# A batched A·Bᵀ kernel: the stores wait for one load more, and the last two batches are stored from the SP queue

## The chip, the cores and the metric

One core of a Trainium2 chip runs the program. The metric is the time of one execution in device microseconds (us); a median of several runs is given.

## The reference

```python
batch, m, k, n = 16, 512, 512, 512          # float32 inputs a, b from randn
def reference(a, b):
    return np.matmul(a, b.transpose(0, 2, 1)).astype(np.float32)
```

33.55 MB are read and 16.78 MB written. The work inside is done in bf16.

## The kernel before

The kernel works on pairs of batches. A load brings `a` or `b` of one pair (2 MB), so there are 16 loads, 0 to 15; a store takes the product of one batch (1 MB), so there are 16 stores, 0 to 15. There are seven slots for loads and seven for outputs (`ob`). VectorE casts to bf16, TensorE transposes and multiplies, ScalarE copies the transposed `a` and the products. SP issues all loads; GpSimd (POOL in the profile) issues all stores, after a first wait for a load.

```python
    STORES = "SSSSOSOSOSSOSOSOSOSOSOSSS"      # S: issue a store; O: wait for one, tell ScalarE
    ...
        for n in range(NL):
            load(n)
        for n in range(2 * pairs):            # SP: relay each landing, issue a later load
            got = nc.sync.wait_ge(s_ld[n % NL], 16 * (n // NL + 1))
            ...
            if n > 0 and n + NL - 1 < 2 * pairs:
                load(n + NL - 1)
        for n in range(batch - NO, batch - 1):
            nc.sync.wait_ge(s_st[n % NO], 16 * (n // NO + 1))

        n_st = n_of = 0
        nc.gpsimd.wait_ge(s_ld[6], 16)        # load 6 has landed: stores may start
        for what in STORES:
            if what == "S":
                slot = n_st % NO
                nc.gpsimd.wait_ge(s_out, n_st + 1)        # ScalarE has copied batch n_st
                nc.gpsimd.dma_start(
                    out[n_st].rearrange("(p j) n -> p j n", j=J), ob[:, slot]
                ).then_inc(s_st[slot], 16)
                n_st += 1
            else:
                nc.gpsimd.wait_ge(s_st[n_of % NO], 16 * (n_of // NO + 1)).then_inc(s_of, 1)
                n_of += 1
    ...
        # ScalarE, per pair: copies of the transposed a, then for each batch e of the pair
                take(s_of, 1)                             # a free slot of ob
                ...                                       # four copies ob <- ps
    ...
    with tc.tile_critical(no_gpsimd_drain=True):
        nc.sync.wait_ge(s_st[(batch - 1) % NO], 16 * ((batch - 1) // NO + 1))
```

Of the kernel before, what the change touches and what calls it, by code (L numbers as in the profile page):

```python
# [10 lines left out]
def kernel(  # L11
# [6 lines left out]
    nc = tc.nc  # L18
    P = 128
    batch, M, K = a.shape  # L20
    _, N, _ = b.shape
    J = M // P
# [7 lines left out]
    NO = 7  # L30


    STORES = "SSSSOSOSOSSOSOSOSOSOSOSSS"

    def sbuf(name, shape, dtype):
        return ctx.enter_context(nc.sbuf_tensor(name, shape, dtype))

    def sem(name):
        return tc.alloc_semaphore(name)

    with tc.tile_critical(no_gpsimd_drain=True):  # L41
# [8 lines left out]
        ob = sbuf("ob", [P, NO, J, N], f32)  # L50
# [3 lines left out]
        s_set = sem("s_set")  # L54
        s_ld = [sem(f"s_ld{i}") for i in range(NL)]
        s_second = [sem(f"s_second{i}") for i in range(2)]
        s_st = [sem(f"s_st{i}") for i in range(NO)]

        s_go = sem("s_go")
# [13 lines left out]
        s_out = sem("s_out")  # L73
# [5 lines left out]
            out=ident[:], in_=ident[:], compare_op=mybir.AluOpType.not_equal, fill=1.0,  # L79
# [7 lines left out]
        def load(n):  # L87
            u, slot = n // 2, n % NL
            src = (a if n % 2 == 0 else b)[2 * u:2 * u + 2].rearrange(
                "e (p j) k -> (e p) j k", j=2 * J  # L90
            )
            if n >= NL:

                nc.sync.wait_ge(s_cd, n - NL + 2)
            if n < 2:
                nc.sync.dma_start(
                    ld[:, slot, :J, :], src[:, :J, :]
                ).then_inc(s_ld[slot], 16)
                nc.sync.dma_start(
                    ld[:, slot, J:, :], src[:, J:, :]  # L100
                ).then_inc(s_second[slot], 16)
            else:
                nc.sync.dma_start(ld[:, slot], src).then_inc(s_ld[slot], 16)
# [3 lines left out]
        for n in range(2 * pairs):  # L107
# [6 lines left out]

            if n > 0 and n + NL - 1 < 2 * pairs:
                load(n + NL - 1)
        for n in range(batch - NO, batch - 1):
            nc.sync.wait_ge(s_st[n % NO], 16 * (n // NO + 1))


        n_st = n_of = 0
        nc.gpsimd.wait_ge(s_ld[6], 16)
        for what in STORES:
            if what == "S":
                slot = n_st % NO
# [20 lines left out]
        with nc.Fori(0, pairs, engines=[dve]) as u:  # L146
            for x, (h, w, s_c, s_w) in enumerate(
# [4 lines left out]
                if x == 0:  # L152
# [3 lines left out]
                    out=h[:, :J, :], in_=src[:, :J, :HK]  # L156
# [4 lines left out]
                    out=h[:, J:, :], in_=src[:, J:, :HK]  # L161
                ).then_inc(s_c, 1)
                nc.vector.tensor_copy(  # L163
                    out=w[:, J:, :], in_=src[:, J:, HK:]
                ).then_inc(s_w, 1)
            for ko in range(KO):
# [5 lines left out]
                if ko == 1:  # L172
# [3 lines left out]
                    out=tb[:, ko, :],  # L176
# [9 lines left out]
        with nc.Fori(0, pairs, engines=[act]) as u:  # L186
            for ko in range(KO):
# [5 lines left out]
                for e in range(2):  # L193
                    c = nc.scalar.copy(  # L194
                        out=ta[:, ko, e * J * P:(e + 1) * J * P].rearrange(
                            "k (j p h) -> k j p h", j=J, h=2
                        ),
# [5 lines left out]
            for e in range(2):  # L203
                take(s_of, 1)
                dst = ob[:, bass.ds((u * 2 + e) % NO, 1)].rearrange("m o j n -> m (o j) n")
                for j in range(J):
                    if j < J - 1:
                        nc.scalar.wait_ge(s_mm, j + 1)
                    else:
# [3 lines left out]
                        out=dst[:, j, :].rearrange("m (p j) -> m p j", j=2 * J),  # L213
# [51 lines left out]


    with tc.tile_critical(no_gpsimd_drain=True):
        nc.sync.wait_ge(s_st[(batch - 1) % NO], 16 * ((batch - 1) // NO + 1))


# [28 lines left out]
```

## Time and profile before

| | before |
|---|---|
| time, median (range) | 126.12 us (125.92 to 126.35) |
| span of the profile | 124.6 us |
| TensorE, VectorE, ScalarE busy | 75%, 56%, 55% |
| transfer rate, mean of the span | 404 GB/s |
| last landing of a store | 123.02 us |

The prediction below shows the rows of the page that carry the argument. The list of waits gives the rest of GpSimd's story; its columns are the total in us, how often, and the longest.

```profile
POOL out_dram L127 <- DMA out_dram<-ob: 59.3, 9, 10.2
POOL out_dram L127 <- DMA ld<-in_a_dram: 36.8, 1, 36.8
POOL out_dram L127 <- ACT ob L212: 10.1, 2, 8.5
```

GpSimd waits once for a load (the hold), then for its own stores, because only four or five may be under way, and at the end twice for ScalarE. That last row is the only place where a store waits for compute.

### The profile page before, as it was taken

The numbers are of one execution on the slowest core, as the hardware profiler recorded it, in microseconds if no ns is written. First come the engines' busy times: TensorE is split into PE (matmuls) and PEld (weight loads), VectorE is DVE, ScalarE is ACT, GpSimd is POOL, SyncE is SP. The second block draws the span as 40 slices with busy tenths as digits, with TensorE's granted clock in tenths as the row PEclk, the third lists the DMA queues.
The fourth block names the chain that finished last, engine by engine and source line by source line (L and its number), as shares of the span: only waits on it lengthen the run. The fifth ranks groups of instructions, "written<-read, shape, count | busy, mean of one in ns | idle before, by whom it ended". The sixth has DMA issues, their size and how long they took to land. (4 is left out here: it accounts for less than half of the span.)

```text
span 124.6 us, 2416 instructions
## 1 busy us (share of the span) xinstructions
PE 93.2 (75%) x768; PEld 58.8 (47%) x768; DVE 70.4 (56%) x112; ACT 68.3 (55%) x130; POOL 10.7 (9%) x22
## 2 busy tenths in 40 slices
PE   0005199998999999899989965999389992899300
PEld 0005295467447644754674445844286451734000
DVE  0055677758983895686689139590687608830000
ACT  4004234589468855956795682645906666456300
POOL 2000000000006200100003020010101001200300
PEclk9999999999999999999999998699959999999995
DMA  3999999999999999999999999999999999999790
GB/s 79 397 437 429 447 426 437 442 421 431 421 426 421 400 442 413 418 447 410 455 410 423 450 402 460 408 426 447 418 437 421 434 413 434 421 423 429 316 381 8
DMA packets 4896, 50.33 MB, mean 404 GB/s; under 512 B 544, under 2 KB 544, under 8 KB 544
## 3 DMA queue, kind: packets, MB, share of 16 engines
q1 hardware_dynamic: 2592, 33.56, 63.9%
q0 software_dynamic: 2304, 16.78, 32.0%
HBM read 33.55 MB, written 16.78 MB: 404 GB/s over the span
## 5 line engine op out<-in xcount | busy, mean ns | idle before, releaser
L254 PE MATMUL ps<-tb,ta 128*128 128x512 bf16 x256 | 57.7, 379 | 0.4
L212 ACT COPY ob<-ps 128x512 f32 x64 | 34.7, 587 | 26.1 <-PE ps L254 26.1
L194 ACT COPY ta<-tp 128x512 bf16<-128x512 bf16 x64 | 32.9, 604 | 21.5 <-PE tp L235 21.5
L254 PEld LDWEIGHTS ps<-tb,ta 128*128 128x128 bf16 x256 | 24.1, 98 | 30.5 <-issue 3.9
L235 PE MATMUL tp<-ident,ha 128*128 128x128 bf16 x256 | 20.8, 241 | 12.6 <-PEq L136 12.6
L235 PE MATMUL tp<-ident,hb 128*128 128x128 bf16 x256 | 19.5, 237 | 10.0 <-PEq L136 9.9
L235 PEld LDWEIGHTS tp<-ident,ha 128*128 128x128 bf16 x256 | 18.2, 109 | 15.6 <-issue 14.0
L175 DVE COPY tb<-tp 128x1024 bf16<-128x1024 bf16 x32 | 21.4, 686 | 5.5 <-DVEq L136 5.4
L235 PEld LDWEIGHTS tp<-ident,hb 128*128 128x128 bf16 x256 | 17.3, 108 | 10.9 <-issue 10.9
L127 POOL DMA_DIRECT2D out_dram<-ob x16 | 10.0, 628 | 106.2 <-DMA out_dram<-ob 59.3
L155 DVE CAST hb<-ld 128x1024 bf16 x8 | 5.6, 699 | 16.8 <-DVEq L136 16.8
L170 DVE COPY ha<-wa 128x2048 bf16<-128x2048 bf16 x8 | 5.5, 694 | 8.0 <-DVEq L136 7.6
L155 DVE CAST ha<-ld 128x1024 bf16 x8 | 5.5, 690 | 6.8 <-DVEq L136 6.7
L160 DVE CAST hb<-ld 128x1024 bf16 x8 | 5.5, 684 | 1.1 <-DVEq L136 1.1
L160 DVE CAST ha<-ld 128x1024 bf16 x8 | 5.5, 686 | 1.0 <-DVEq L136 1.0
L174 DVE COPY hb<-wb 128x2048 bf16<-128x2048 bf16 x8 | 5.5, 686 | 0.5 <-DVEq L136 0.5
L158 DVE CAST wb<-ld 128x1024 bf16 x8 | 5.6, 694 | 0.0
L158 DVE CAST wa<-ld 128x1024 bf16 x8 | 5.5, 688 | 0.0
L163 DVE CAST wa<-ld 128x1024 bf16 x8 | 5.5, 687 | 0.0
L163 DVE CAST wb<-ld 128x1024 bf16 x8 | 5.5, 684 | 0.0
L185 ACT ACT_TABLE_LOAD x1 | 1.3, 1283 | 1.1 <-SPq L41 1.1
L78 POOL TENSOR_SCALAR_AFFINE_SELECT ident<-ident 128x128 bf16<-128x128 bf16 x1 | 0.3, 284 | 0.2 <-POOL ident L76 0.2
(6 smaller groups left out, 0.8 us busy)
## 6 DMA issues: line engine op xcount, KB each, us to landing
out_dram<-ob POOLq DMA_DIRECT2D x16, 1024.0 KB, 23.9
ld<-in_a_dram SPq DMA_DIRECT2D x7, 2048.0 KB, 33.0
ld<-in_b_dram SPq DMA_DIRECT2D x7, 2048.0 KB, 33.7
ld<-in_a_dram SPq DMA_DIRECT2D x2, 1024.0 KB, 6.3
ld<-in_b_dram SPq DMA_DIRECT2D x2, 1024.0 KB, 10.4
```

What stands on the lines that cost most here:

```text
L127: nc.gpsimd.dma_start(out[n_st].rearrange("(p j) n -> p j n", j=J), ob[:, slot]).then_inc(s_st[slot], 16)
L155: nc.vector.tensor_copy(out=h[:, :J, :], in_=src[:, :J, :HK]).then_inc(s_cd, 1)
L158: nc.vector.tensor_copy(out=w[:, :J, :], in_=src[:, :J, HK:])
L160: nc.vector.tensor_copy(out=h[:, J:, :], in_=src[:, J:, :HK]).then_inc(s_c, 1)
L163: nc.vector.tensor_copy(out=w[:, J:, :], in_=src[:, J:, HK:]).then_inc(s_w, 1)
L170: nc.vector.tensor_copy(out=ha[:], in_=wa[:]).then_inc(s_ca, 1)
L174: nc.vector.tensor_copy(out=hb[:], in_=wb[:]).then_inc(s_cb, 1)
L175: nc.vector.tensor_copy(out=tb[:, ko, :], in_=tp[:, 2 + ko % 2].rearrange("k j p -> k (j p)"),).then_inc(s_eb, 1)
L194: c = nc.scalar.copy(out=ta[:, ko, e * J * P:(e + 1) * J * P].rearrange("k (j p h) -> k j p h", j=J, h=2), in_=tp[:, ko % 2, :, e * HP:(e ...
L212: c = nc.scalar.copy(out=dst[:, j, :].rearrange("m (p j) -> m p j", j=2 * J), in_=ps[:, j, :].rearrange("m (j p) -> m p j", j=2 * J),)
L235: t = nc.tensor.transpose(tp[:, 2 * x + g, j, :], h[:, j, g * P:(g + 1) * P], ident[:])
L254: t = nc.tensor.matmul(ps[:, j, :], ta[:, ko, (e * J + j) * P:(e * J + j + 1) * P], tb[:, ko, :].rearrange("k (j p) -> k j p", j=2 * J)[:, ...
```

## The change

It has two parts. The hold is lengthened from load 6 to load 7 (slot 0 used a second time, so its semaphore stands at 32). Loads then run longer without stores beside them, the last load should come earlier, and so should the last product. And the last two stores leave GpSimd's queue for SP's, each with a semaphore of its own.

```diff
-    STORES = "SSSSOSOSOSSOSOSOSOSOSOSSS"
+    STORES = "SSSSOSOSOSSOSOSOSOSOSOS"
+    LAST = 2
...
+        s_last = [sem(f"s_last{i}") for i in range(LAST)]
...
-        for n in range(batch - NO, batch - 1):
+        for n in range(batch - LAST, batch):
+            nc.sync.wait_ge(s_out, n + 1)
+            nc.sync.dma_start(
+                out[n].rearrange("(p j) n -> p j n", j=J), ob[:, n % NO]
+            ).then_inc(s_last[n % LAST], 16)
+        for n in range(batch - NO, batch - LAST):
             nc.sync.wait_ge(s_st[n % NO], 16 * (n // NO + 1))
+        for n in range(batch - LAST, batch - 1):
+            nc.sync.wait_ge(s_last[n % LAST], 16)
...
-        nc.gpsimd.wait_ge(s_ld[6], 16)
+        nc.gpsimd.wait_ge(s_ld[0], 32)
...
-        nc.sync.wait_ge(s_st[(batch - 1) % NO], 16 * ((batch - 1) // NO + 1))
+        nc.sync.wait_ge(s_last[(batch - 1) % LAST], 16)
```

## The prediction

> **What bounds the kernel now.** I read the page by slices first, because a change of stores is worth nothing if the transfer engines are not the limit. The first two rows below give, in 40 equal slices of 3.1 us, the busy tenths of the sixteen transfer engines and the GB/s moved; the others are the two queues (q1 carries the loads that SP issues, q0 the stores that GpSimd issues) and the total.
>
> ```profile
> DMA  3999999999999999999999999999999999999790
> GB/s 79 397 437 429 447 426 437 442 421 431 421 426 421 400 442 413 418 447 410 455 410 423 450 402 460 408 426 447 418 437 421 434 413 434 421 423 429 316 381 8
> ...
> q1 hardware_dynamic: 2592, 33.56, 63.9%
> q0 software_dynamic: 2304, 16.78, 32.0%
> HBM read 33.55 MB, written 16.78 MB: 404 GB/s over the span
> ```
>
> The transfer engines are full from about 2 us to the end, except in the first slice and slices 37 and 38 (316 and 381 GB/s, 115 to 121 us). TensorE by contrast is busy 75%. So the time is bytes over rate, plus a start, plus holes. I then asked for chosen stretches; the last two columns are the busy share of the transfer engines and GB/s.
>
> ```profile
> 2.00:38.00 36.00, 24.29 (x192) 15.88 (x193) 22.68 (x36) 16.27 (x33) 0.00 (x0) 1.00 1.01 421
> 44.00:100.00 56.00, 50.20 (x402) 31.32 (x401) 37.28 (x60) 35.53 (x68) 4.67 (x8) 0.94 1.01 428
> 104.00:115.00 11.00, 8.97 (x75) 5.31 (x76) 5.61 (x10) 5.86 (x12) 0.87 (x1) 1.00 1.01 425
> 115.50:116.25 0.75, 0.75 (x4) 0.14 (x2) 0.00 (x0) 0.30 (x1) 0.19 (x1) 1.00 0.09 33
> ```
>
> Loads alone, loads with stores, and stores alone all move 421 to 428 GB/s with the engines full: the order of loads and stores does not change the rate. The one hole is 0.75 us at 115.5 us, where the engines are 9% busy. Its cause is in the timeline of GpSimd's end (start, duration, and in brackets the wait before it):
>
> ```profile
> 102.61 0.53 POOL L127 DMA_DIRECT2D out_dram<-ob  x1 [6.61 <-DMA out_dram<-ob]
> 105.83 0.87 POOL L127 DMA_DIRECT2D out_dram<-ob  x1 [2.69 <-DMA out_dram<-ob]
> 115.16 0.53 POOL L127 DMA_DIRECT2D out_dram<-ob  x1 [8.45 <-ACT ob L212]
> 117.33 0.53 POOL L127 DMA_DIRECT2D out_dram<-ob  x1 [1.65 <-ACT ob L212]
> ```
>
> Stores 14 and 15 are issued when ScalarE has copied them, at 115.16 and 117.33. Store 13 had been issued at 105.83 and most engines ran out of it at 115.5 to 115.75; the first packet of store 14 starts at 116.28, 1.1 us after its issue. The chain of waits that the page prints stops at such a transfer and credits the end to TensorE (6%); taken alone it would mislead.
>
> A finer reading moderates this. Each transfer adds to its semaphore sixteen times, once per engine, and the trace has each time. **One engine of the sixteen lags**: for load 6, before any store, the last increment comes 0.11 us after the next to last; for load 10, 0.44; load 15, 1.14; store 10, 1.57; store 13, 1.83 (116.25 and 118.08); then store 14, 1.21 and store 15, 1.08. This engine goes on from store 13 (118.08) to 14 (120.53) to 15 (123.02) at 2.45 and 2.49 us each, which is the pace of eight packets of 0.31 us: it had no hole. The hole belongs to the fifteen others, and the slow one sets the end at 123.02.
>
> [...] 67% and 34% of the engines for q1 and q0 between 44 and 100 us, sum 101%. [...] load packets are 16 KB, store packets 8 KB, and between 44 and 100 us the bytes are 15.99 and 7.99 MB, two to one. [...]
>
> **The change part by part.**
> 1. *The hold.* GpSimd waits for load 7 instead of load 6. Load 6 lands at 38.19 in the trace and load 7 at 43.40. The first store, issued at 38.49, has its first packet at 42.34, when load 7 has run out (its last packets start at 41.72). Loads alone take 4.89 us each, loads beside stores 7.32, stores alone 2.45. So stores now begin near 42.34 + 4.9 = 47.2, load 8 lands near 48.3 instead of 50.75, and every later load about 2.45 us earlier (load 15 at 100.5 instead of 103.00). No byte is saved: one store moves from before load 15 to after it.
> 2. *What it gives.* From pair 5 on, compute waits for loads (TensorE starts the products of pairs 5, 6 and 7 at 80.4, 94.9 and 109.0, at the pace of two loads, where pairs 1 to 4 came every 11.5). So the last pair comes 2.45 earlier: store 14 is issued at about 112.7 and store 15 at 114.9. Work through store 13 ends where it did, near 115.6 on the fifteen engines, so store 14 is in its queue some 1.8 us before they run dry. The hole is closed: at most 0.75 us, for these fifteen.
> 3. *The SP queue.* It replaces two issues of 0.53 us on GpSimd by two of about 0.33 on SP (a load's issue there), both off the path once the hole is closed. SP has by then issued its last load (59.28) and relayed the last landing, so it is free. Stores 12 and 13 on q0 then share packets with 14 and 15 on q1, which delays 12 and 13 and no one waits for them. Two of sixteen stores leave q0. If the lag is made by q0 at 1.83/14 = 0.13 us per store, this is worth up to 0.25 us on the slow engine; store 14 and 15 themselves showed little more lag, so perhaps 0.1 to 0.2.
> 4. *Output buffers.* Store landings come 4.9 us later until loads end, and ScalarE must wait for a slot. Batch 9 needs store 2 (65.61 + 4.9 = 70.5; wanted at 70.8), batch 11 store 4 (85.1; wanted at 85.5 - 2.45 = 83.1), batch 13 store 6 (99.8; wanted at 97.7). I expect two new waits of some 2 us on ScalarE. They fall on the second batch of a pair; afterwards ScalarE had 2.6 to 3.2 us of idle before its next copies, and the four copies no longer wait for TensorE between them. So these should be absorbed, and 1 us of delay would still leave store 14 in time.
>
> Sum: the fifteen engines end some 0.7 us earlier, the slow one 0.1 to 0.3 us earlier, and the slow one counts. 126.12 - 0.3 = **125.8 us**.
>
> **Rivals.**
> (a) *The hole is the bound after all.* If the slow engine's lag is a debt that goes away with q0's last stores, the end moves by the whole hole and part of the lag: 0.75 + 0.3, about 125.1. For it: slices 37 and 38 lose about 0.8 and 0.35 us of full rate. Against: the even 2.45 us steps of the slow engine.
> (b) *Nothing.* Transfers stay full on the engine that counts, total bytes are equal, 126.1. For it: the same rate in all mixtures, and the steps again. This is close to my own view.
> (c) *Slots become the wait.* If stores start later than 47.2, waits on ScalarE grow past their slack, the last pair is not earlier, and a hole opens again: 126.5 to 127.5. For it: batches 9, 11 and 13 have no margin. Against: ScalarE is busy only 55% and TensorE has idle before pairs 5, 6 and 7 (it waits for loads).
> (d) *Two queues of stores at the end cost rate*, or the slow engine lags more: up to 0.5 us. Against: 428 GB/s with both queues in use.
>
> **Range and chances.** The floor is bytes over rate: 50.33 MB at 428 GB/s is 117.6 us, from a first packet at 1.95 to 119.6, then about 0.5 to land and 1.6 from the last landing (123.02) to the end of the span (124.6): 121.7 in the span, 123.2 in the measured time, which was 1.5 above the span. Even this ideal is hardly 2.3% below, and it needs the lag gone as well. Slower by 2.5 us would need a stall that the slack cannot take. Range 125.0 to 126.6; faster by over 2%: 0.02, within 2%: 0.95, slower by over 2%: 0.03.
>
> **What would show it.** Step 1: GpSimd's first store after 43.4, load 15 landing near 100.5. Step 2: last issues near 112.7 and 114.9, no slice under 400 GB/s between 112 and 118 us. Step 3: two store issues on SP; the last landing near 122.8, with one engine an instant of 1 us or more behind fifteen that finish near 121.3. Step 4: ScalarE waits for out transfers of about 2 us at two places, TensorE's last product no later than 114. The prediction is wrong if load 15 lands before 99.5 or after 102, if the last landing is below 122.2, or if the slow engine's lag at the end is under 0.7 us.

The sum, 0.1 to 0.3 us on the slow engine, 126.12 - 0.3 = 125.8 us, is worked out from the trace of the kernel before, and its weakest term, 0.13 us per store on q0, is an estimate from the lag of 1.83 us at store 13. That stores 14 and 15 would share packets with 12 and 13 is taken from the stretch of 44 to 100 us, where the packet records have 976 load packets of 16 KB on q1 and 975 store packets of 8 KB on q0. And "once per engine" can be followed in the packet records of the changed kernel: from 115.2 us on, packets that follow each other end to start make sixteen rows, and stores 14 and 15 have eight packets of 8 KB and one increment of 4 bytes each in every row.

## The result

| | before | changed |
|---|---|---|
| time, median of 6 (range) | 126.13 us (125.92 to 126.39) | 125.84 us (125.62 to 125.99) |
| span of the profile | 124.61 us | 124.07 us |
| last landing of a load | 103.00 us | 100.22 us |
| last landing of a store | 123.02 us | 122.71 us |
| next to last of its sixteen increments | 121.94 us | 120.97 us |
| from the last landing to the end of the span | 1.59 us | 1.36 us |

The ratio is 0.9972, with a 95% interval of 0.9956 to 0.9988. A ratio here is the mean time of one kernel's fast runs over that of the other's in the same rounds, so it is not quite the ratio of the medians.

The page of the changed kernel, the same rows as in the prediction (transfer engines by slice, GB/s by slice, the queues):

```profile
DMA  4999999999999999999999999999999999999980
GB/s 79 401 428 431 452 423 438 423 428 423 433 433 423 428 433 396 433 407 449 417 428 449 409 441 425 420 441 420 449 415 417 428 431 428 425 425 423 428 338 11
...
q1 hardware_dynamic: 2880, 35.65, 68.2%
q0 software_dynamic: 2016, 14.68, 28.1%
HBM read 33.55 MB, written 16.78 MB: 406 GB/s over the span
```

The dip at slice 37 (316 GB/s before) is gone: 428. Two stores, 2.10 MB, have moved from q0 to q1. The same stretches as before, of the changed kernel (the last two columns are the busy share of the transfer engines and GB/s):

```profile
44.00:100.00 56.00, 51.68 (x425) 31.52 (x424) 37.01 (x60) 35.87 (x69) 6.15 (x11) 0.97 1.01 427
104.00:115.00 11.00, 9.17 (x64) 4.79 (x64) 2.89 (x5) 6.39 (x12) 0.53 (x1) 1.00 1.01 427
115.50:116.25 0.75, 0.00 (x0) 0.00 (x0) 0.00 (x0) 0.00 (x0) 0.00 (x0) 1.00 1.04 437
```

Where the engines were 9% busy for 0.75 us, they are now full, and the other rates are as they were. So 15 of the 16 engines finish 0.97 us earlier, yet the span ends only 0.54 us earlier and the time 0.3 us. The timelines of SP and of ScalarE in the changed kernel (start, duration, and in brackets the wait before; a q after an engine's name means its instruction queue) answer to the steps of the prediction; each view has its own fence:

```profile
112.11 2.52 SPq L122 DMA_DIRECT2D out_dram<-ob  x2
```

```profile
84.86 2.05 ACT L222 COPY ob<-ps 128x512 f32 x4 [3.19 <-ACTq L146]
...
99.54 2.06 ACT L222 COPY ob<-ps 128x512 f32 x4 [2.81 <-PE ps L264]
```

Store 14 is issued at 112.11, three us earlier than before (115.16), and store 15 some two us after it; the view merges the two and their wait. ScalarE has the two new waits, at batches 11 and 13, and no others. The profile puts the second down to TensorE; store 6, whose slot it needs, landed at 99.24.

One row that I had not looked at before predicting is in the list of instructions of the program's last line. It is GpSimd's DRAIN, here of the kernel before (durations are least, median and longest in ns, then the first and last start):

```profile
L294 POOLq DRAIN  x3: 34/118/2834, 120.9 to 124.3; - x3
```

and here of the changed kernel:

```profile
L304 POOLq DRAIN  x3: 34/117/1204, 120.6 to 123.8; - x3
```

The trace has the times. Before, the drain starts at 120.89, when SP has seen store 14 land, and ends at 123.72, which is 0.70 us after store 15 landed. SP is at the final meeting of the engines at 123.51, and all wait for GpSimd. In the changed kernel the drain runs from 120.58 to 121.78, before store 15 has landed, and nobody waits for it: the end comes 1.36 us after the last landing, not 1.59. That is 0.23 us of the gain.

The other 0.31 us of the spans' difference is the last landing. But the two executions differed before any store was issued: load 6 landed at 38.19 and 37.91. Counted from load 6, the last store lands 84.83 us later before and 84.80 after. What the lagging engine has to do took the same time.

### The profile page after: what moved, and what is told of

Its sections match the earlier page's. It is cut to its first block, busy times and chain, and to the rows that moved or that the text cites. A ratio compares the mean times of both kernels' runs of the same rounds, so it can differ in the third digit from the quotient of the medians.

```text
span 124.1 us, 2416 instructions
## 1 busy us (share of the span) xinstructions
PE 92.3 (74%) x768; PEld 57.8 (47%) x768; DVE 70.2 (57%) x112; ACT 68.1 (55%) x130; POOL 9.5 (8%) x20
## 5 line engine op out<-in xcount | busy, mean ns | idle before, releaser
L245 PE MATMUL tp<-ident,ha 128*128 128x128 bf16 x256 | 20.2, 236 | 12.5 <-PEq L146 12.5
L245 PEld LDWEIGHTS tp<-ident,ha 128*128 128x128 bf16 x256 | 17.5, 107 | 15.7 <-issue 14.0
L137 POOL DMA_DIRECT2D out_dram<-ob x14 | 8.8, 631 | 95.7 <-DMA out_dram<-ob 54.3
```

The source lines that it names most:

```text
L137: nc.gpsimd.dma_start(out[n_st].rearrange("(p j) n -> p j n", j=J), ob[:, slot]).then_inc(s_st[slot], 16)
L245: t = nc.tensor.transpose(tp[:, 2 * x + g, j, :], h[:, j, g * P:(g + 1) * P], ident[:])
```

## The experiments

The question was what the 0.3 us are made of. Four accounts stood against each other. **S**: one engine sets the end and had no hole, so the hold alone gives nothing. **H**: the holes of the fifteen cost time. **Q**: each store that leaves GpSimd's queue relieves the lagging engine. **D**, formed after the first runs: it is GpSimd's drain.

All kernels gave correct results. This table has the profiled executions of those that I compare below; "from load 6" is from the last increment of load 6 to the last landing of a store, in us.

```
kernel        last store's queue  last landing  from load 6  landing to end  drain, longest
before        GpSimd              123.02        84.83        1.59            2.83
hold alone    GpSimd              122.74        84.71        1.59            2.83
SP alone      SP                  122.83        84.84        1.36            1.20
changed       SP                  122.71        84.80        1.36            1.20
 second look  SP                  122.68        84.68        1.36            1.20
 third look   SP                  122.73        84.66        1.36            1.20
only 14 on SP GpSimd              122.70        84.60        1.55            2.18
only 15 on SP SP                  122.90        84.98        2.54            1.29
seven on SP   SP                  122.79        84.69        1.41            0.80
ScalarE queue SP                  122.71        84.64        1.35            0.10
```

### The changed kernel, more rounds

No edit. The first run:

> The changed kernel once more, in more rounds, to size the gain. Theory (the one lagging engine sets the end and has no hole before the change): 125.8 us, 0.2 to 0.4 under before (ratio 0.997 to 0.9985). Rival (the first result was noise): ratio 1.000 within 0.1%.

Measured: 125.79 us against 126.24 (ratio 0.9959, 0.9945 to 0.9972). A later call:

> The changed kernel a third time, on the chip of this call, for the next kernel to be held against and for the spread of its gain from call to call: ratio 0.996 to 0.998, 125.7 to 125.95 us.

Measured: 125.82 against 126.16 (0.9976, 0.9963 to 0.9989). With the first result (0.9972) the gain is real, and 0.2% to 0.4%; all three intervals exclude 1.

### The hold alone

```diff
-        nc.gpsimd.wait_ge(s_ld[6], 16)
+        nc.gpsimd.wait_ge(s_ld[0], 32)        # nothing else changed from before
```

> Stores held until load 7, all sixteen stores still from GpSimd. Theory: store 14 is issued near 112.5, no hole on any engine, the fifteen engines finish near 121, and the slow one near 122.7 to 122.9; time 125.8 to 126.0. If the gain of the change came from the two stores leaving q0, this one loses it: 126.1. If it came from the order of loads and stores, this has all of it: 125.8.

Measured: 126.22 us against 126.24; ratio 0.9996 (0.9984 to 1.0008). The hole did close; the stretch that was 9% busy, now in this kernel:

```profile
115.50:116.25 0.75, 0.00 (x0) 0.00 (x0) 0.00 (x0) 0.00 (x0) 0.45 (x1) 1.00 0.99 415
```

A hole of 0.75 us on fifteen engines was removed and the time did not move. H falls. The time of store 15's last increments says why: the fifteenth at 121.05 (before: 121.94), the sixteenth at 122.74 (before: 123.02; 0.16 us of the difference is that load 6 landed earlier).

### SP alone

```diff
-        nc.gpsimd.wait_ge(s_ld[0], 32)
+        nc.gpsimd.wait_ge(s_ld[6], 16)        # the rest as in the changed kernel
```

> The last two stores from SP, stores held until load 6 as before. Theory: store 14 is still issued near 115.1, so fifteen engines keep a hole of 0.3 to 0.8 us, but the slow engine has none: 125.9 to 126.2 and the lag at the end about 1 us. If the gain came from the two stores leaving q0, 125.8. If holes on the fifteen cost time, 126.1 or more.

Measured: 125.98 us against 126.24; ratio 0.9977 (0.9964 to 0.9990). The hole is there, exactly as before:

```profile
115.50:116.25 0.75, 0.75 (x5) 0.38 (x4) 0.00 (x0) 0.54 (x2) 0.00 (x0) 1.00 0.09 33
```

So the queue of the last stores gave 0.3 us with the hole open. "From load 6" is 84.84, as before, and what shortened is the end, 1.36 instead of 1.59 us. This is where account D came from. The changed kernel was another 0.2 us faster (125.79), although the hold alone gave 0.06 by the means (126.23 against 126.29). Some 0.15 us of the hold's worth in company with SP is not explained.

### The stores let go earlier

```diff
-        nc.gpsimd.wait_ge(s_ld[6], 16)
+        nc.gpsimd.wait_ge(s_ld[5], 16)        # nothing else changed from before
```

> The kernel before with the stores let go one load EARLIER, after load 5. Theory: load 15 lands 2.45 us later (105.5), store 14 is issued near 117.6 and its first packet near 118.7, while the slow engine runs out of store 13 near 117.6: a hole of about 1.1 us on the engine that counts, so 127.0 to 127.4. Rival (total bytes alone decide): 126.1. Rival (every us of hole on the fifteen counts): 128.5.

Measured: 128.21 us (127.37 to 128.73), ratio 1.0152 (1.0122 to 1.0182). The profiled run took 127.44. Its stretches show the hole:

```profile
115.50:116.25 0.75, 0.75 (x6) 0.30 (x4) 0.00 (x0) 0.17 (x1) 0.00 (x0) 1.00 0.11 44
116.25:118.00 1.75, 1.75 (x10) 0.78 (x8) 0.00 (x0) 1.07 (x2) 0.53 (x1) 1.00 0.02 9
118.00:118.50 0.50, 0.34 (x2) 0.00 (x0) 0.00 (x0) 0.46 (x1) 0.00 (x0) 1.00 0.63 262
```

Fifteen engines stand still from about 115.7 to 118.34, when the first packet of store 14 starts. Load 15 landed at 105.08, store 14 was issued at 117.24. The lagging engine finished store 13 at 117.62, and then had to wait too: at store 14 and store 15 all sixteen increments lie together (the last 0.02 and 0.04 us behind the next to last), and the last landing is 124.04, 1.02 us later than before. So in these runs the lag was slack for the other fifteen: the hole of 0.75 us, beside a lag of 1.83 us at store 13, was free, and this one of 2.6 us, which outlasted the lag, was not. That is what account S says, and the estimate of 1.1 us came close for this run.

This hole also shows that it is one engine, and how it lags. The packet records of the kept trace (no view prints them one by one) have a single engine at work from 115.9 to 117.14: four packets of 8 KB that took 0.31 to 0.34 us. Between 104 and 115 us 95% of the store packets took 0.309. The engine loses its time packet by packet.

Four of the six runs took 128.1 to 128.7; I have no trace of one of them, and why they are a further us longer is open.

### Only one of the two stores on SP

Two kernels, both with the hold of the changed kernel:

```diff
-    STORES = "SSSSOSOSOSSOSOSOSOSOSOS"
-    LAST = 2
+    STORES = "SSSSOSOSOSSOSOSOSOSOSOSS"       # only 15 on SP
+    LAST = 1
```

> The changed kernel, but only store 15 from SP and store 14 from GpSimd. Theory D (the gain of the change is GpSimd's drain at the end, which lasted 0.70 us beyond the last landing where the last store was GpSimd's, and put the span's end 1.59 instead of 1.36 us after that landing): drain is over before store 15 lands, so the whole gain stays: 125.8 us, end 1.36 us after the last landing. Theory Q (each store off q0 saves lag): half the gain, 126.0.

```diff
-        for n in range(batch - LAST, batch):
+        for n in range(batch - LAST, batch - 1):          # only 14 on SP
...
+        nc.gpsimd.wait_ge(s_out, batch)
+        nc.gpsimd.dma_start(
+            out[batch - 1].rearrange("(p j) n -> p j n", j=J), ob[:, (batch - 1) % NO]
+        ).then_inc(s_last[1], 16)
```

> The changed kernel, but only store 14 from SP and store 15 from GpSimd. Theory D: the drain waits for store 15, the end is 1.59 us after the last landing, the gain is lost: 126.1 to 126.25. Theory Q: half the gain, 126.0, as with store 15 alone.

With only store 14 on SP: 126.12 us against 126.23; ratio 0.9992 (0.9979 to 1.0005). The gain is lost, as D expected and Q did not. The drain again lasts until 0.66 us after store 15's landing (122.70):

```profile
L309 POOLq DRAIN  x3: 34/117/2182, 121.2 to 124.0; - x3
```

With only store 15 on SP the six runs fall in two groups: 125.69, 125.98 and 125.99, which keep the whole gain, and 126.99, 127.00 and 127.25 (ratio of all 1.0006, 0.9972 to 1.0040). Neither account had foreseen the second. The profiled run is of that group:

```profile
L304 POOLq DRAIN  x3: 34/125/1286, 123.3 to 125.2; - x3
```

Store 15, on its own queue, landed at 122.60, and store 14, behind store 13 on GpSimd's queue, at 122.90. SP waits for store 14 before the drain may start, so the drain began only at 123.26 and its 1.29 us lay bare; the end came 2.54 us after the last landing. Of the faster group I have no trace; that store 14 lands early enough there is an inference. The drain is thus a piece of work that can be hidden behind the last store's transfer or not. Moving two stores hid it (1.36 us from the last landing to the end); moving the wrong one (1.55), or one only (2.54 in the profiled run), did not do so safely.

### More stores off GpSimd's queue

Seven stores (9 to 15) from SP:

```diff
-    STORES = "SSSSOSOSOSSOSOSOSOSOSOS"
-    LAST = 2
+    STORES = "SSSSOSOSOSSOSOOOOO"
+    LAST = 7
```

> The changed kernel with the last seven stores (9 to 15) from SP instead of the last two. Theory Q (each store on GpSimd's queue costs the lagging engine about 0.1 us[...]): lag at the end near 1.3 instead of 1.7, time 125.4. Theory B (the lagging engine is only slower for its bytes in this phase, whichever queue): lag 1.7, time 125.8 as with two. If the drain at the end is the whole of what SP gives, 125.8 as well.

And none on GpSimd: stores 0 to 13 from ScalarE's queue, one pair later each, with ScalarE's loop unrolled.

```diff
-        nc.gpsimd.wait_ge(s_ld[0], 32)        # and GpSimd's dma_start
+        def store(n):
+            if n == 0:
+                nc.scalar.wait_ge(s_ld[0], 32)
+            nc.scalar.wait_ge(s_out, n + 1)
+            nc.scalar.dma_start(
+                out[n].rearrange("(p j) n -> p j n", j=J), ob[:, n % NO]
+            ).then_inc(s_st[n % NO], 16)
...
-        with nc.Fori(0, pairs, engines=[act]) as u:
+        for u in range(pairs):
...
+            for n in (() if u < 2 else range(0 if u == 2 else 2 * u - 2, 2 * u)):
+                store(n)
```

> The changed kernel with stores 0 to 13 issued from ScalarE's queue (its loop unrolled, each store issued one pair later), 14 and 15 from SP, and no transfer from GpSimd at all. Theory Q: no engine lags (the spread of a transfer's sixteen landings stays under 0.9 us, as in the loads before any store), the last landing is near 121.2, time 124.2 to 124.6. Theory B: one engine still lags by 1.5 us or more, 125.7 to 125.9. If issuing on ScalarE delays its copies enough to open a hole at the end, 126 or more.

Measured: seven on SP 126.01 us against 126.19, ratio 0.9984 (0.9970 to 0.9998); ScalarE's queue 125.93 against 126.19, ratio 0.9987 (0.9972 to 1.0001). In the second no transfer uses q0 any more:

```profile
q1 hardware_dynamic: 2880, 35.65, 68.3%
q10 hardware_dynamic: 2016, 14.68, 28.1%
```

Still one engine lags: by 1.54 us at store 15 with seven on SP and by 1.31 us with none on GpSimd; and the last landing, 122.79 and 122.71, is what it was. What changed with the queues is how early the fifteen others are. (A growth of the lag that the first expectation named, and from which it worked out its 1.3 us, isn't in the changed kernel's trace: the lag there is 1.48 us at store 9 and 1.74 at store 15. The 0.9 us of the second stands above what the same trace shows for the loads before any store, sixteen landings within 0.70 to 0.74 us; before the change they lay within 1.07 to 1.09.) Q falls: the lagging engine's time belongs to the engine, not to GpSimd's queue. The packet records agree: between 104 and 115 us 30 of 571 store packets took longer than 0.310 us before (0.328 on average), and 28 of 574 with no store on GpSimd (0.326). That is about one engine's share of sixteen. Neither kernel beats the changed one by its ratio; they have the drain's gain (1.41 and 1.35 us from landing to end) and nothing further.

The two kernels also show how the drain's length went with the number of GpSimd's stores, once these had landed. Here it is with seven stores on SP, and with none on GpSimd:

```profile
L304 POOLq DRAIN  x3: 34/129/796, 120.7 to 123.9; - x3
```

```profile
L306 POOLq DRAIN  x3: 34/41/103, 120.6 to 123.8; - x3
```

The first of the three drains, the one meant throughout, took 0.04 us when GpSimd had issued no store, 0.80 after nine, 1.20 after fourteen (in all seven profiles of such kernels) and 1.29 after fifteen (only 15 on SP). An estimate from these figures is 0.08 us for each store that it issued.

### The stores held longer still

```diff
-        nc.gpsimd.wait_ge(s_ld[0], 32)
+        nc.gpsimd.wait_ge(s_ld[1], 32)        # load 8; the rest as in the changed kernel
```

> The changed kernel with stores held by one load more still, until load 8. Theory S: total work per engine is unchanged and the tail has no hole to close, so 125.8 unless ScalarE stalls. Store 0 lands near 60.4, and ScalarE waits near 1 us for it, 4 us for stores 2 and 4, 4 us for store 6; the last pair then is no earlier than in the changed kernel. If those waits push store 14's issue past 115.5, a hole opens again: 126.2 to 127.

Measured: 126.16 us against 126.23; ratio 0.9990 (0.9977 to 1.0003). ScalarE's waits for a slot grew from one listed wait of 3.2 us to

```profile
ACT ob L222 <- ACTq L146: 11.0, 3, 4.5
```

and store 14's issue moved to 114.18, two us later than in the changed kernel, although load 15 landed at 97.76. There is still no hole at 115.5, and the end is 1.36 us after the last landing. That landing came at 122.99, 84.99 us from load 6, and I cannot say what the further 0.2 us are. The hold has no more to give, and the slots begin to cost.

### Less work for the lagging engine

If one engine sets the end, taking bytes from it should move the end by more than all of the above. The sixteen engines cannot be named from the records, so I let the shape of store 15 choose: cut into pieces, it may fall on them unevenly. A whole store gave each engine eight packets (stores 14 and 15 of the changed kernel); how a piece is spread no run had shown. First, 120 + 8 partitions:

```diff
...
+                nc.sync.dma_start(dst[:120], ob[:120, n % NO]).then_inc(s_last[n % LAST], 16)
+                nc.sync.dma_start(dst[120:], ob[120:, n % NO]).then_inc(s_tail, 16)
...
```

> The changed kernel, store 15 cut in two on SP: 120 partitions [...] and the last 8 partitions [...]. Theory S (one engine lags by 1.7 us and sets the end): if it [...] has no part in store 15 and ends with store 14 near 120.2; [...] the last landing is near 121.4 to 121.6 and the time 124.6 to 124.9. If the lagging engine [...] has more to do: last landing 123.1 to 123.2, time 126.2 to 126.3. If the end isn't set by one engine, 125.8 to 126.1.

Then 96 + 21 + 7 + 4:

```diff
...
+            cuts = (0, P) if n < batch - 1 else (0, 96, 117, 124, P)
+            for lo, hi in zip(cuts, cuts[1:]):
+                nc.sync.dma_start(
+                    dst[lo:hi], ob[lo:hi, n % NO]
+                ).then_inc(s_last[n % LAST], 16)
...
```

> The changed kernel with store 15 cut on SP into 96, 21, 7 and 4 partitions. [...] Theory S7 (the lagging engine that sets the end [...]): it has two packets of 0.31 us less, so the last landing goes from 122.7 to about 122.1, the lag shrinks to some 0.2 us, and the time is 125.2 to 125.4. If the lagging engine [...] has 2 or 3 more: last landing 123.3 to 123.6, 126.4 to 126.8. If the end is not one engine's matter, 125.8 to 126.1.

The two expectations are estimates for either case, that the pieces leave the lagging engine less to do or more; in packets of 0.31 us, the figure of the trace.

Measured: the first took 126.75 us (126.14 to 126.98), ratio 1.0037 (1.0015 to 1.0058), with the last landing at 123.06; the second 127.40 us, ratio 1.0115 (1.0095 to 1.0136), last landing 123.98. Both made it worse; by the packet records both gave the lagging engine more, not less. The times lie above what was expected if it got more; the profiled runs took 126.31 and 127.17, the low end of each, and I have no trace of the longer ones. The end moved by 0.35 and 1.27 us, the first about as expected if the lagging engine got more, the second 0.4 us beyond the highest expectation.

The 8-partition piece has nine updates, one at its issue and eight landings, of which seven come from 121.03 to 122.13 and the last at 123.06. In the second kernel the last two increments, 123.68 and 123.98, are 0.30 us apart, one packet. The packet records have the engine that ends last close with three packets and an increment, then one packet and an increment, then nothing. From the order of issue I take these for shares of the pieces of 21 and of 7, with none of the piece of 4; that is an inference.

If the piece of 96 gave it six packets, at the rate of eight for a whole store of 128, it had two more than in the changed kernel: by this estimate about 0.6 us of the 1.27, at 0.31 us a packet. The rest I put down to slow packets: one of its store 14 took 0.83 us, and that store landed 0.41 us later than in the changed kernel; one of its store 15 took 0.58 us instead of 0.31. After 115 us 13 store packets of the first kernel and 11 of the second took over 0.4 us, and none in any other run. The cut itself came with slow packets, so these two runs don't price a packet cleanly. That less work for this engine would bring the end earlier is not shown: both cuts gave it more. If the piece of 4 left it out, more such pieces might. The changed kernel stays the fastest of those that ran.

## Why the prediction was right, and where it was not

The time was right: 125.8 said, 125.84 measured, and within 2% as said.

**Steps that held.** *Step 1*: load 15 landed at 100.22 (100.5 said); the first packet of store 0 started at 47.06 (47.2 said). *Step 2*: store 14 was issued at 112.11 (112.7 said); the hole closed and fifteen engines finished at 120.97 (121.3 said) while the last landing was at 122.71 (122.8 said). *Step 4*: ScalarE waits at batches 11 and 13 and nowhere else, 3.2 and 2.8 us where "some 2 us" was said, and they were absorbed: TensorE's last products start at 106.19, 2.78 us earlier than before. *Rival (a)*, that the hole was the bound, was rejected for the right reason, and the hold alone (ratio 0.9996) shows it.

**The step that failed is the third.** It put the worth of the SP queue at "up to 0.25 us on the slow engine", because "the lag is made by q0 at 1.83/14 = 0.13 us per store", and held the two issues themselves to be off the path. The lag at the end did not shrink; it grew, from 1.08 to 1.74 us, as the others finish earlier. With no store on GpSimd at all, the last landing was the same, 122.71. The term for the slow engine measures zero where two kernels differ in this alone: from load 6 to the last landing it is 84.84 us with SP alone against 84.83 before, and 84.66 to 84.80 in the changed kernel against 84.71 with the hold alone. In its place stands a term that I did not have: GpSimd's drain, 0.23 us. The span's tail of 1.6 us was in the prediction as a constant ("1.6 from the last landing to the end of the span"), and I did not ask what was in it. So the sum came out right by luck: one wrong term was of about the right size.

A smaller error in the same step: stores 14 and 15 were to share packets with 12 and 13. On fifteen engines they did not. Store 14 was issued at 112.11, but SP's first store packet started at 115.34, when store 13 was running out. Only the lagging engine shared, and there store 13's last increment came at 119.61 instead of 118.08.

Three figures in the prediction are off, and its central number rests on none of them. Its floor took 1.5 us from span to measured time, which sets a median against the span of another run; of the same run it is 1.8, so the floor is 123.5 us. Store landings came 4.3 us later, not 4.9 (store 4 at 84.56 instead of 80.24; 4.6 later counted from load 6). And 41.72 for the start of load 7's last packets isn't in the trace: the packet records have them from 40.93 on.

**What stays open.** The changed kernel's gain was 0.24% to 0.41%, and the drain is 0.23 of 126.2 us, 0.18%. The rest, some 0.1 to 0.3 us, belongs to the hold in company with SP, or to the spread; no single experiment holds it. A hint, but no proof: from load 6 to the last landing it is 84.60 to 84.80 us in the seven profiles that hold the stores until load 7, leave store 15 whole and land it last, and 84.83 and 84.84 in the two that hold them until load 6. And why one engine's packets take longer, once stores are under way, is not known.

## What to carry to other kernels

Before closing a hole in the transfers, look at all sixteen increments of a transfer, not at the mean busy share: where one engine lagged by 1.83 us, a hole of 0.75 us on the others cost nothing (the hold alone: 0.9996). Read what happens between the last landing and the end of the span as carefully as the rest; the queues of the last two stores decided whether GpSimd's drain was hidden (1.36 us instead of 1.59 in this kernel). And a prediction that hits is not yet a reason: taking the change apart cost four kernels and showed that half of it did nothing alone.
